# Four gate column units of a streaming encoder step moved from the attention's filling into the paired projection stage

## The chip, the core and the metric

The kernel runs on one core of a Trainium2 chip. The metric is the device time of one launch in microseconds (us). Three runs of the kernel before gave 999.62, 1000.45 and 1001.2 us; the median is 1000.45 us.

## What is computed

One layer of a streaming encoder works on 1024 prompt frames and 64 sample frames (1088 tokens in all) of width 1024. Cut to what matters here:

```python
h = rms_norm(x, norm_w) @ w_in                        # 6144 columns
sq, sk, sv, sz, cq, ck, cv, cz, g_sb, g_cb = split(h)
o_sb = stick_breaking(sq, sk, sv)                     # 8 heads x 64, causal
o_cb = band_attention(norm(cq), norm(ck), cv, bias)   # 8 heads x 64, band of 640 keys
b_sb = (o_sb * silu(sz)) @ w_proj_sb
b_cb = (o_cb * silu(cz)) @ w_proj_cb
y = x + (sigmoid(g_sb) * b_sb + sigmoid(g_cb) * b_cb) @ w_out
```

The two gates g_sb and g_cb have 1024 columns each: columns 4096 to 5119 and 5120 to 6143 of w_in. The weights of the stick-breaking branch (sb) come from a product over the keys that are nearer, those of the band branch (cb) from a softmax over at most 640 keys.

## The kernel before, in words

All tensors are float32. A product of two float32 tensors is done as three matmuls on float32r halves: high by high, high by low and low by high. The helper `Weights` (lines 98 to 130) makes the two halves of a weight block: ScalarE copies the high half (L115), GpSimd subtracts to get the low half (L122).

The order of the work is written out by hand, and every engine takes its instructions in that order. The stages are:

1. **Natural stage** (L464): the columns of cb q, cb k, and both v, with tokens as output rows.
2. **Paired stage** (L593 to L658, matmuls at L634): for each entry of `pairs`, two blocks of 128 columns by all 1088 tokens, in the manner of Strassen and Winograd. The tokens are halved (544 each), the 1024 rows of w_in are halved (512 each), and the two column blocks are the third pair of halves. Seven products of quarters (`right` lists their token operands, some of them sums prepared beforehand in `tms`) stand for the eight of the plain way. `presum` (L389) makes weight sums on VectorE, `prep` (L415) makes the halves (ScalarE L433, GpSimd L434), `emit` (L565) evicts a finished quarter. Each product takes 24 matmuls: 4 blocks of rows, 3 halves, and two pieces of 256 and 288 tokens. So a pair takes 168 matmuls. There are 8 pairs: 4 for sb q and k and 4 of the kind "silu" for z. The kind "sig" is known to `emit`, with a sigmoid by ScalarE and a store by SyncE, and no pair uses it.
3. **Attention**: 144 steps listed in `seq`: branch sb then cb, 4 head pairs p each, tiles t = 8 (the sample), 0 to 7, and two heads hd. The columns of both gates are 16 plain **units** of 128 columns. The generator `run_fill` (L766) issues their matmuls one by one (L773): 3 token chunks of 384, 384 and 320, 8 blocks of rows, 3 halves, 72 matmuls a unit. `fill(n)` takes n matmuls from it. After the units the generator goes on with the sb output projection (`proj_sb`, L873), of which a part is issued within the attention and the rest behind it.
4. **Output**: rest of the sb projection, cb projection (L917), last product (L1409).

One attention step i does, in this order: `qk(i)`, 2 or 4 score matmuls (L1024, L1025) and what reads them; half of the step's fill; `av` (L1115), the product with v, at the steps behind the second head of an odd t or of t = 8; `tr(i - 3)` (LAG is 3), transposes of the weights by TensorE (L1076) into two `pt` buffers, emptied by ScalarE (L1085) or VectorE (L1087) in turn; `mid(i)`; the other half of the fill.

In sb, `qk` lets ScalarE make two sigmoids (L1027, L1028), and `mid` is a scan (L1044) and a product (L1045) on VectorE. In cb, `qk` lets VectorE add the bias to the scores and keep the extreme (L1030, one or two halves), then ScalarE take the exponential with a row sum (L1034); `mid` takes the reciprocal (L1047) and scales (L1048) on VectorE. So in cb VectorE needs ScalarE's exponential of step i before it can finish step i, and in program order it takes up step i + 1 only then.

How many fill matmuls a step gets is planned at L1160 to L1190: six times 24 are issued ahead of the first step; `n_sb` and `n_cb` are then spread over the steps of a branch by weights of n for sb and n + 150 for cb, with n the number of keys of the step. In cb 24 more are given at p = 0, t = 8. For each unit, its weights are split (L115, L122) at the start of the second chunk of the unit before it.

Of the kernel before, what the change touches and what calls it, by code (L numbers as in the profile page):

```python
# [10 lines left out]
AF = mybir.ActivationFunctionType  # L11
# [6 lines left out]
KT = 8  # L18
# [14 lines left out]
def hybrid_step_kernel(ctx: ExitStack, tc: tile.TileContext, x_prompt, x_sample, c_sbk, c_sbv, c_cbk, c_cbv,  # L33
# [47 lines left out]
    d_g = {b: [dram.tile([128, T], F32, name=f"d_g{b}{u}") for u in range(KT)] for b in ("sb", "cb")}  # L81
# [63 lines left out]
    pairs = []  # L145
    for p in (0, 2):
        pairs += [("k", 512 + 128 * p, p), ("q", 128 * p, p)]
    for p in (0, 2):
        pairs += [("silu", 1536 + 128 * p, d_z["sb"][p:p + 2]), ("silu", 3584 + 128 * p, d_z["cb"][p:p + 2])]
    units = [("ev_act", 4096 + 128 * j, (AF.Sigmoid, d_g["sb"][j])) for j in range(KT)]  # L150
    units += [("ev_act", 5120 + 128 * j, (AF.Copy, d_g["cb"][j])) for j in range(KT)]

    def put_t(dst, src):
# [1004 lines left out]
        flush()  # L1158
        f()
    FP = 180  # L1160
    n_sb = 72 * 7
    n_cb = 72 * (len(units) - 9) + FP
    wt = {"sb": lambda n: n, "cb": lambda n: n + 150}
    tot = {b: sum(wt[b](band(b, t)[1]) for bb, p, t, hd in seq if bb == b) for b in ("sb", "cb")}
    amount = {"sb": n_sb, "cb": n_cb}
# [329 lines left out]
```

## Time and profile before

| What | us |
|---|---|
| median of 3 runs | 1000.45 |
| profiled execution, span from first to last instruction | 1000.1 |
| paired stage, 226.65 to 399.06 | 172.4 |
| six fills ahead of the first step, 399.06 to 422.6 | 23.5 |
| attention, sb, 422.6 to 626.2 | 203.6 |
| attention, cb, 626.2 to 846.0 | 219.8 |
| TensorE busy in the whole span | 977.8 |
| VectorE busy | 657.0 |
| ScalarE busy | 472.9 |
| GpSimd busy | 324.9 |

The profile lists no time of the profiled execution besides its span; the span lies 0.35 us under the median of the runs. In the profile PE is TensorE's matmul, PEld its weight load, DVE VectorE, ACT ScalarE, POOL GpSimd and SP SyncE. A matmul's row lists its start and a modelled length that overlaps the next, so the price of a matmul is the distance between starts, or a stretch of the chain divided by its count.

### The profile page before, as it was taken

The numbers are of one execution on the slowest core, as the hardware profiler recorded it, in microseconds if no ns is written. First come the engines' busy times: TensorE is split into PE (matmuls) and PEld (weight loads), VectorE is DVE, ScalarE is ACT, GpSimd is POOL, SyncE is SP. The second block draws the span as 40 slices with busy tenths as digits, with TensorE's granted clock in tenths as the row PEclk, the third lists the DMA queues.
The fourth block names the chain that finished last, engine by engine and source line by source line (L and its number), as shares of the span: only waits on it lengthen the run. The fifth ranks groups of instructions, "written<-read, shape, count | busy, mean of one in ns | idle before, by whom it ended". The sixth has DMA issues, their size and how long they took to land.

```text
span 1000.1 us, 20177 instructions
## 1 busy us (share of the span) xinstructions
PE 977.8 (98%) x7512; PEld 930.8 (93%) x7512; DVE 657.0 (66%) x1233; ACT 472.9 (47%) x1075; POOL 324.9 (32%) x338
## 2 busy tenths in 40 slices
PE   5999999999999999999999999999999899999998
PEld 5999999999999999988898888898989798999998
DVE  5456674895455454099898878565766766499735
ACT  5534443444344433277676656454445434365320
POOL 3276663215445543211111101110202200386552
PEclk9999999999999999999999999999999999999999
DMA  7726577424656332786566544765656854773642
GB/s 237 224 92 221 189 249 256 150 91 150 198 155 192 102 97 85 188 228 187 146 166 159 160 114 117 206 200 152 193 150 186 253 168 147 242 224 101 196 136 89
DMA packets 180865, 169.83 MB, mean 170 GB/s; under 512 B 34912, under 2 KB 167136, under 8 KB 180640
## 3 DMA queue, kind: packets, MB, share of 16 engines
q1 hardware_dynamic: 172048, 160.23, 54.2%
q10 hardware_dynamic: 8720, 8.33, 2.6%
q8 instruction: 59, 0.97, 0.4%
q14 instruction: 38, 0.31, 0.1%
HBM read 109.78 MB, written 58.72 MB: 168 GB/s over the span
## 4 chain that ended last, share of the span: by engine, by line
PE 92%; DMA 2%; DVE 2%; ACT 1%; SPq 1%; issue 1%; POOL 1%; DVEq 0%; ACTq 0%
PE acc L464 19%; PE acc L773 18%; PE b L634 17%; PE b L1409 8%; PE o L1115 7%; PE pt L1076 6%; PE b L917 5%; PE z L1025 3%; PE z L1024 3%; PE acc L873 3%; PE pk L349 1%; DMA wrawx<-in_w_in_dram 1%; DMA gt<-d_gsb 1%; DVE be L1045 1%; PE pt L277 1%
## 5 line engine op out<-in xcount | busy, mean ns | idle before, releaser
L122 POOL TENSOR_TENSOR wlo<-wraw,whi 128x1024 fp32r<-128x1024 f32 x30 | 74.2, 2473 | 243.9 <-ACT whi L115 209.2
L773 PE MATMUL acc<-xm,whi 128*128 128x384 f32 (+1 forms) x384 | 128.5, 335 | 0.0
L1044 DVE TENSOR_TENSOR_SCAN kp<-kp,imp 64x576 f32<-64x576 f32 (+8 forms) x72 | 102.8, 1427 | 21.3 <-ACT kp L1027 21.1
L1034 ACT ACTIVATE be<-be,sm 128x640 f32<-128x640 f32 (+5 forms) x72 | 50.8, 705 | 97.1 <-DVE sm L1030 97.1
L1076 PE MATMUL pt<-ident,be 128*128 128x128 f32 (+2 forms) x608 | 90.1, 272 | 6.4 <-DVE wT L1087 3.4
L1085 ACT ACTIVATE wT<-pt 128x512 f32<-128x512 f32 (+3 forms) x130 | 63.6, 502 | 55.1 <-PE pt L1076 55.1
L1076 PEld LDWEIGHTS pt<-ident,be 128*128 128x128 f32 (+2 forms) x608 | 68.5, 140 | 18.4 <-issue 6.4
L464 PE MATMUL acc<-whi,xa 128*128 128x256 f32 x256 | 74.2, 292 | 0.0
L773 PEld LDWEIGHTS acc<-xm,whi 128*128 128x128 f32 x384 | 72.5, 189 | 1.1
L464 PE MATMUL acc<-wlox,xm 128*128 128x256 f32 x256 | 70.8, 278 | 0.0
L464 PE MATMUL acc<-whi,xm 128*128 128x256 f32 x256 | 70.8, 278 | 0.0
L464 PE MATMUL acc<-wlo,xa 128*128 128x256 f32 x256 | 70.7, 278 | 0.0
L464 PE MATMUL acc<-whix,xb 128*128 128x256 f32 x256 | 70.7, 278 | 0.0
L464 PE MATMUL acc<-whix,xm 128*128 128x256 f32 x256 | 70.6, 278 | 0.0
L1115 PE MATMUL o<-wT,vp 128*64 128x256 f32 (+1 forms) x608 | 66.7, 359 | 0.0
L1045 DVE TENSOR_TENSOR be<-be,kp 64x576 f32<-64x576 f32 (+8 forms) x72 | 60.3, 837 | 9.6
L1027 ACT ACTIVATE kp<-z 128x384 f32<-128x384 f32 (+6 forms) x112 | 54.3, 485 | 24.4 <-PE z L1025 22.9
L773 PE MATMUL acc<-xa,wlo 128*128 128x384 f32 (+1 forms) x192 | 65.4, 341 | 0.0
L773 PE MATMUL acc<-xa,whi 128*128 128x384 f32 (+1 forms) x192 | 65.3, 340 | 0.0
L773 PE MATMUL acc<-xm,wlo 128*128 128x384 f32 (+1 forms) x192 | 65.1, 339 | 0.0
L1115 PEld LDWEIGHTS o<-wT,vp 128*64 128x64 f32 x608 | 42.5, 137 | 23.7 <-issue 7.6
L773 PE MATMUL acc<-xb,whi 128*128 128x384 f32 (+1 forms) x192 | 64.0, 333 | 0.0
(298 smaller groups left out, 3017.2 us busy)
## 6 DMA issues: line engine op xcount, KB each, us to landing
wraw<-in_w_in_dram SPq DMA_DIRECT2D x35, 512.0 KB, 4.7
wrawx<-in_w_in_dram SPq DMA_DIRECT2D x13, 512.0 KB, 4.4
sq<-d_qsbT SPq DMA_DIRECT2D x32, 192.0 KB, 4.7
sq<-d_qcbT SPq DMA_DIRECT2D x32, 192.0 KB, 3.7
gt<-d_gsb SPq DMA_DIRECT2D x30, 192.0 KB, 2.7
xt<-in_x_prompt_dram SPq DMA_DIRECT2D x8, 512.0 KB, 5.1
d_kcbT<-hl SPq DMA_DIRECT2D x8, 512.0 KB, 4.5
d_qcbT<-hl SPq DMA_DIRECT2D x8, 512.0 KB, 5.6
```

Of the source, the lines that this page charges most:

```text
L122: (eng or G).tensor_tensor(out=l, in0=raw, in1=h[:].bitcast(F32), op=OP.subtract)
L464: TE.matmul(ps, x, w, start=m == 0, stop=m == len(steps) - 1)
L634: TE.matmul(ps[:, :m], w[:, hl_, k], right[s](x)[:, k, a:b], start=s < 3 and k == 0 and e == 0, stop=k == 3 and e == 2, skip_group_check=s ...
L773: TE.matmul(ps[:, :b - a], w[:, k], xk(x, k)[:, a:b], start=k == 0 and n == 0, stop=k == KT - 1 and n == 2)
L1027: A.activation(kp[:r, x:y], z[:r, :m], AF.Sigmoid, scale=-0.125)
L1034: A.activation(be[:r, :n], be[:r, :n], AF.Exp, bias=kp[:r, j:j + 1], scale=-1.0, accum_out=kp[:r, 2:3])
L1044: V.tensor_tensor_scan(kp[:r, n - 1::-1], kp[:r, n - 1::-1], im[:, ::-1], 0.0, op0=OP.mult, op1=OP.add)
L1045: V.tensor_tensor(out=be[:r, :n], in0=be[:r, :n], in1=kp[:r, 1:n + 1], op=OP.mult)
L1076: TE.transpose(pt[:kr, x, :r], be[:r, kb * 128:kb * 128 + kr], ident[:r, :r])
L1085: A.activation(w[:, sl:sl + m, q0:q0 + r], pt[:, :m, :r], AF.Copy)
L1115: TE.matmul(o[hd * 64:hd * 64 + 64, c0:c1], vv[:kr, kb, hd * 64:hd * 64 + 64], wT[b, p, j, hd, s // 4][:kr, s % 4, c0:c1], start=si == 0, ...
L1409: TE.matmul(ps[:, t], left[s](xs_, k)[:, ts_], wt_[:, k], start=s < 3 and t == k == e == 0, stop=k == 3 and e == 2, skip_group_check=s > 2 ...
```

## The change

The first four gate units, columns 4096 to 4607 (g_sb, the sigmoid gates j = 0 to 3), become two pairs of the kind "sig" behind the 8 pairs. 12 units are left. The shares of the fill follow: ahead of the first step 144 as before; in sb 36 x 13 = 468 for 504; in cb 72 x 10 - 468 + 180 = 432 for 684. FP stays at 180, so as many matmuls of the sb projection are issued within the attention as before.

```diff
-    units = [("ev_act", 4096 + 128 * j, (AF.Sigmoid, d_g["sb"][j])) for j in range(KT)]
+    NG = 4
+    pairs += [("sig", 4096 + 128 * j, d_g["sb"][j:j + 2]) for j in range(0, NG, 2)]
+    units = [("ev_act", 4096 + 128 * j, (AF.Sigmoid, d_g["sb"][j])) for j in range(NG, KT)]
     units += [("ev_act", 5120 + 128 * j, (AF.Copy, d_g["cb"][j])) for j in range(KT)]
...
     FP = 180
-    n_sb = 72 * 7
-    n_cb = 72 * (len(units) - 9) + FP
+    n_sb = 36 * (len(units) + 1)
+    n_cb = 72 * (len(units) - 2) - n_sb + FP
```

## The prediction

> **What bounds the kernel now.** I read the page first: the span, the busy shares and the chain that ended last.
>
> ```profile
> span 1000.1 us, 20177 instructions
> ...
> PE 977.8 (98%) x7512; PEld 930.8 (93%) x7512; DVE 657.0 (66%) x1233; ACT 472.9 (47%) x1075; POOL 324.9 (32%) x338
> ...
> PE 92%; DMA 2%; DVE 2%; ACT 1%; SPq 1%; issue 1%; POOL 1%; DVEq 0%; ACTq 0%
> ```
>
> TensorE is busy nearly always, and 92% of the chain is its own work. On this reading alone, any saved matmul is saved time. But the change moves work between stages, so I read each stage next (columns: stretch, length, busy time and count of PE, PEld, DVE, ACT and POOL, granted clock, DMA share, GB/s). The first four rows are the stages, the fifth is one pair of heads in cb (its 18 steps), the sixth about one in sb.
>
> ```profile
> 226.65:399.06 172.41, 172.41 (x1385) 171.55 (x1385) 89.14 (x174) 68.41 (x159) 82.67 (x56) 1.00 0.46 140
> 399.06:422.60 23.54, 23.54 (x145) 23.54 (x144) 2.16 (x5) 5.16 (x9) 5.72 (x6) 1.00 0.64 174
> 422.60:626.20 203.60, 200.10 (x1436) 178.27 (x1435) 173.94 (x187) 137.91 (x336) 24.39 (x76) 0.99 0.62 162
> 626.20:846.00 219.80, 216.13 (x1570) 195.21 (x1567) 144.11 (x463) 102.82 (x249) 32.83 (x32) 1.00 0.65 185
> ...
> 681.28:733.99 52.71, 52.71 (x391) 48.01 (x389) 34.29 (x111) 24.46 (x61) 5.60 (x6) 1.00 0.62 170
> ...
> 478.50:529.00 50.50, 50.50 (x365) 44.93 (x365) 43.91 (x49) 34.75 (x86) 6.25 (x20) 1.00 0.62 159
> ```
>
> In the paired stage VectorE, ScalarE and GpSimd each work half the time or less: TensorE alone sets the pace. In sb VectorE is at 85%. In cb it is at 66%, which looks like room. Whether it is room decides this case.
>
> **The paired stage: what is added.** The chain of waits in order of time has two long unbroken stretches of TensorE (start, length, what, count).
>
> ```profile
> 300.67 98.39 PE b L634 x792
> 399.06 23.73 PE acc L773 x144
> ```
>
> A paired matmul costs 98.39 / 792 = 0.1242 us, a plain one 23.73 / 144 = 0.1648 us. Per column of tokens (272 and 362.7 on average) both are 0.456 and 0.454 ns, so seven products for eight is a true saving of TensorE's time. Two pairs are 2 x 168 = 336 matmuls, or **+41.7 us**. Upper bound: an eighth of the stage row, 21.55 a pair, or 43.1; it holds transposes of k that a gate pair has not. Behind the matmuls lie, per pair, 7 splits by ScalarE and GpSimd, 4 sums and some ten evictions by VectorE, two loads of 512 KB and the gate's stores; the eight pairs already did the same at POOL 82.67 of 172.41 and a DMA share of 0.46, so I cost them at nothing. Without that cover the price would be what the busiest of them exceeds TensorE by, and none comes near. The last pairs' stores on SP's queue now stand ahead of the first attention loads; those have 23.5 us of fill as cover as before. Four unit loads, four splits and 12 evictions with their stores leave the attention.
>
> **The attention: what is removed.** Four units are 288 plain matmuls, 288 x 0.1648 = 47.5 us if TensorE paces every step: 36 in sb (5.9 us) and 252 in cb (41.5 us). All in all that would be 47.5 - 41.7 = 5.7 us gained. So what counts is whether TensorE still paces.
>
> *sb, 36 fewer of 504.* Half a matmul a step. In the sb row TensorE waits 203.60 - 200.10 = 3.5 us; VectorE's steps lie close under it (43.91 of 50.50). Its lag is let run over several steps and is caught up at the long av products. Bounds: nothing gained, and 5.9. I take **-3.5**, above the middle, since the row shows TensorE with next to no wait.
>
> *cb, 252 fewer of 684.* A pair of heads now has 684 / 4 = 171 fills; it will have 432 / 4 = 108. TensorE's own work falls from 52.7 to 52.7 - 63 x 0.165 = 42.3 us a pair. Now the other engines. First, TensorE's step at t = 7 today:
>
> ```profile
> 672.45 0.31 PE L1024 MATMUL z<-ks,sq 128*128 128x320 f32 x1
> ...
> 675.67 0.31 PE L1024 MATMUL z<-ks,sq 128*128 128x320 f32 x1
> ...
> 677.39 2.38 PE L1115 MATMUL o<-wT,vp 128*64 128x256 f32 x24
> ```
>
> One step without av is 675.67 - 672.45 = 3.22 us, with 12 fills. It will have 12 x 432 / 684, 7 to 8: about 2.4 us. Second, the step of VectorE and ScalarE, at a place where both were behind, so that nothing in it waits for TensorE:
>
> ```profile
> 721.46 0.48 DVE L1030 CUSTOM_DVE_ANT_0 be<-z,bias 128x320 f32<-128x320 f32 x1
> ...
> 722.75 0.83 ACT L1034 ACTIVATE be<-be,sm 128x640 f32<-128x640 f32 x1 [3.60 <-DVE sm L1030]
> ...
> 723.58 0.58 ACT L1085 ACTIVATE wT<-pt 128x512 f32<-128x512 f32 x1
> 723.70 0.16 DVE L1047 RECIPROCAL sm<-sm 128x1 f32<-128x1 f32 x1 [0.85 <-ACT be L1034]
> 723.90 0.55 DVE L1048 TENSOR_SCALAR be<-be,sm 128x640 f32<-128x640 f32 x1
> 724.37 0.48 DVE L1030 CUSTOM_DVE_ANT_0 be<-z,bias 128x320 f32<-128x320 f32 x1
> ```
>
> This is a **loop between two engines**: VectorE's two reductions, ScalarE's exponential, for which VectorE sits idle 0.85 us, reciprocal, scaling, and only then the next step. It takes 724.37 - 721.46 = 2.91 us however idle the two look in the stage row. Today it hides under 3.22; it doesn't hide under 2.4. The same loop for the other t, by the distance between the first reductions of two steps (t = 8, 8, 0, 0; then t = 1, 2 and 3):
>
> ```profile
> 681.74 0.45 DVE L1030 CUSTOM_DVE_ANT_0 be<-z,bias 64x288 f32<-64x288 f32 x1 [0.21 <-PE z L1025]
> ...
> 684.42 0.44 DVE L1030 CUSTOM_DVE_ANT_0 be<-z,bias 64x288 f32<-64x288 f32 x1
> ...
> 687.09 0.28 DVE L1030 CUSTOM_DVE_ANT_0 be<-z,bias 128x128 f32<-128x128 f32 x1
> ...
> 688.56 0.28 DVE L1030 CUSTOM_DVE_ANT_0 be<-z,bias 128x128 f32<-128x128 f32 x1
> ...
> 639.62 0.42 DVE L1030 CUSTOM_DVE_ANT_0 be<-z,bias 128x256 f32<-128x256 f32 x1 [0.34 <-PE z L1025]
> ...
> 641.37 0.42 DVE L1030 CUSTOM_DVE_ANT_0 be<-z,bias 128x256 f32<-128x256 f32 x1
> ...
> 750.10 0.56 DVE L1030 CUSTOM_DVE_ANT_0 be<-z,bias 128x384 f32<-128x384 f32 x1 [0.43 <-PE z L1025]
> 751.98 0.55 DVE L1030 CUSTOM_DVE_ANT_0 be<-z,bias 128x384 f32<-128x384 f32 x1
> ...
> 702.04 0.68 DVE L1030 CUSTOM_DVE_ANT_0 be<-z,bias 128x512 f32<-128x512 f32 x1
> ...
> 704.21 0.68 DVE L1030 CUSTOM_DVE_ANT_0 be<-z,bias 128x512 f32<-128x512 f32 x1
> ```
>
> 2.68, 1.47, 1.75, 1.88 and 2.17 us. Over a pair of heads: 8 x 2.91 + 2 x (2.68 + 1.47 + 1.75 + 1.88 + 2.17) = **43.2 us**, already more than TensorE's 42.3. The two don't overlap freely: at each av step the loop must wait for TensorE (VectorE's product with z comes behind av), and TensorE may run ahead only until it needs a `pt` buffer, which ScalarE empties behind the exponential. So I add up blocks that end at an av step: lag behind av (0.5), loops of the steps before the last one without av, from that one's reduction to the end of ScalarE's copy (2.7 at 640 keys: 721.46 to 723.58 + 0.58), av (24 in 2.38, 0.1 each), transposes 0.5, half the fill. For t = 6, 7: 0.5 + 2 x 2.91 + 2.7 + 2.4 + 0.5 + 0.6 = 12.5; t = 4, 5 with 16 av: 11.7; t = 8, 0: 0.5 + 2 x 2.68 + 1.4 + 2.4 + 0.5 + 0.2 = 10.4; t = 1 with the 20 short av of the sample, which I put at 1.0: 0.5 + 1.7 + 1.0 + 0.5 = 3.7; t = 2, 3: 0.5 + 2 x 1.88 + 2.1 + 0.8 + 0.9 = 8.1. Together 46.4 us a pair. (For the last step without av at t = 0, 1 and 3 I put its loop, 1.4, 1.7 and 2.1, as an estimate.)
>
> GpSimd's splits come on top, since VectorE now paces:
>
> ```profile
> 675.35 1.11 DVE L1048 TENSOR_SCALAR be<-be,sm 128x640 f32<-128x640 f32 x1
> ...
> 790.56 2.38 POOL L122 TENSOR_TENSOR wlo<-wraw,whi 128x1024 fp32r<-128x1024 f32 x1 [3.81 <-ACT whi L115]
> 790.69 2.60 DVE L1048 TENSOR_SCALAR be<-be,sm 128x640 f32<-128x640 f32 x1
> ```
>
> The scaling of 0.55 us takes 1.11 or 2.60 beside a split: 0.56 to 2.05 us lost each. Of ten splits in cb six are left, 1.5 a pair at 1.3 in the middle: 1.9 us. (The Trainium skill, "SBUF — State Buffer", section "SBUF: two separate sides", has GpSimd and VectorE take one port pair as an exclusive lock for a whole instruction. By it a split could cost 2.4, the pair 3.6 us and the sum 7 us more; the first row speaks for less.) So a pair goes from 52.7 to 48.3, and four give **-17.6**. Bounds: no coupling, 43.2 + 1.5 x 0.56 = 44.0 a pair, -34.8; on the other side 46.4 + 1.5 x 2.05 = 49.5, -12.8; and -41.5 if TensorE paces.
>
> **Sum** against the profiled span: 1000.1 + 41.7 - 3.5 - 17.6 = 1020.7; the median of the runs lies 0.35 higher. Rounded: **1021 us**. Bounds of the terms: 41.7 - 5.9 - 34.8 = +1 and 43.1 - 0 - 12.8 = +30.
>
> **Rivals.** *Loop and TensorE overlap nearly freely*: four `be` buffers and a lag of three steps let TensorE run ahead, 44.0 a pair. That gives +41.7 - 3.5 - 34.8 = +3.4, 1004 us, with a spread of 1002 to 1009. For it: waits of TensorE in cb are few today:
>
> ```profile
> DVE sm L1047 <- ACT be L1034: 16.7, 34, 1.1
> ...
> PE pt L1076 <- ACT wT L1085: 2.0, 2, 1.3
> ...
> PE z L1024 <- DVE sm L1030: 1.4, 2, 1.0
> ```
>
> Against it: those are just the two couplings named, and they show already.
>
> *Faster: TensorE paces cb to the end.* The mechanism is fill as pure surplus: it holds if the loop takes 2.4 us or less a step at 640 keys, in place of 2.91. Then the 5.7 us are gained: 994.4, or 995 by the median. For it speaks the page (98%, 92%); against it the loop's rows.
>
> *The clock falls in the small gaps.* Once before TensorE stood still for 2.40 us, behind a copy that VectorE was late with, and then the clock went down:
>
> ```profile
> 575.38 1.70 PE L1076 MATMUL pt<-ident,be 128*128 128x128 f32 x8 [2.40 <-DVE wT L1087]
> ...
> 574.00:577.50 3.50, 2.12 (x11) 2.12 (x12) 3.37 (x5) 0.98 (x2) 0.29 (x4) 0.74 0.32 95
> ...
> 577.50:580.00 2.50, 2.50 (x17) 1.49 (x18) 0.60 (x2) 0.66 (x3) 0.20 (x2) 0.68 0.00 0
> ```
>
> That cost 0.26 x 3.5 + 0.32 x 2.5 = 1.7 us. Two of the five blocks of each pair with the widest waits and the six splits make 14 such places, 24 us: 1045. Against it: waits of 1.3 and 1.0 left the cb row's clock at 1.00. (The Trainium skill, "TensorE: Matmul & The Clock Gate", section "A second HAM failure mode: psum-queue depth-cycling", says that frequent short idles can make the clock swing; by the section before it only gaps over some 3.4 us do. The 2.40 us here contradict that bound; that short ones swing it no row here shows.)
>
> *The change doesn't do what it says.* Nothing of it depends on data, and the counts follow from the code; what is left is that the seven products are no cheaper, which the price per column excludes. It would leave the time where it is.
>
> **Chances.** My forecast (1010 to 1031) 0.65, free overlap 0.17, TensorE paces 0.08, clock 0.07, nothing 0.03. The range 1003 to 1031 takes in the forecast and nearly all of free overlap and leaves out the rest. A measurement here tells about 0.2% (2 us) from no change. Faster 0.08 (TensorE paces), same 0.05 (nothing, and the low edge of free overlap), slower 0.87.
>
> **What the profile after would show.** Right: the paired stage longer by 41.7 us; sb shorter by up to 5.9; cb some 202 us, not 178; the first reductions at 640 keys 2.9 us apart where no av stands between; TensorE's waits in cb for `pt` (ACT L1085) and for `z` (DVE L1030) grown from 3.7 us to some 25; fewer POOL splits. Wrong: cb at 180 and VectorE still waiting for scores (faster); cb at 185 with its waits at av only (free overlap); a granted clock under 1.00 in many stretches of cb (clock).

## The result, and the profile after

Four runs of the kernel after gave 1015.8 to 1018.47 us, median 1016.93; before, in the same comparison, 1000.83. The ratio is 1.0169 with a 95% interval of 1.0156 to 1.0183: 1.7% slower, where 1021 was forecast. The page of the profile after:

```profile
span 1015.8 us, 20366 instructions
...
PE 983.9 (97%) x7560; PEld 928.0 (91%) x7560; DVE 667.2 (66%) x1261; ACT 479.6 (47%) x1093; POOL 334.3 (33%) x348
...
PE 80%; DVE 8%; DMA 3%; ACT 3%; issue 3%; SPq 2%; POOL 0%; DVEq 0%; ACTq 0%
```

The busy share of TensorE (PE) hardly moved, 98 to 97%, though 15.7 us of span were lost. The third line tells more: TensorE's share of the chain that ended last fell from 92 to 80%, and VectorE (DVE), ScalarE (ACT) and "issue", time in which an engine waited for nothing that the profile shows, took most of its place.

By stages, before and then after. To compare like with like, sb runs from its first score matmul to cb's first, and cb from there to the start of the cb projection; so this cb holds the rest of the sb projection too. Columns as in the prediction.

```profile
226.65:399.06 172.41, 172.41 (x1385) 171.55 (x1385) 89.14 (x174) 68.41 (x159) 82.67 (x56) 1.00 0.46 140
422.63:621.07 198.44, 194.94 (x1403) 173.16 (x1401) 171.83 (x186) 136.19 (x334) 24.39 (x76) 0.99 0.63 164
621.07:865.30 244.23, 239.45 (x1722) 216.84 (x1720) 152.14 (x476) 110.21 (x261) 37.87 (x36) 1.00 0.64 184
...
733.99:789.46 55.47, 54.14 (x391) 48.80 (x389) 36.20 (x114) 28.28 (x71) 11.60 (x12) 1.00 0.65 189
```

```profile
226.07:439.95 213.88, 213.88 (x1722) 213.02 (x1721) 107.87 (x204) 84.17 (x194) 102.25 (x70) 1.00 0.44 134
463.52:658.32 194.80, 190.45 (x1367) 166.94 (x1364) 172.24 (x186) 135.53 (x334) 23.65 (x76) 0.99 0.62 163
658.32:881.00 222.68, 209.60 (x1470) 180.07 (x1469) 144.51 (x476) 101.98 (x246) 28.84 (x32) 0.99 0.65 183
713.77:762.10 48.33, 45.88 (x328) 39.15 (x327) 32.82 (x112) 26.11 (x65) 9.02 (x9) 1.00 0.68 193
762.10:811.79 49.69, 46.23 (x329) 39.11 (x326) 35.78 (x123) 23.55 (x60) 5.91 (x8) 1.00 0.78 216
```

The paired stage took 41.5 us more, sb 3.6 less, cb 21.6 less. The last two rows are the second and the third pair of heads in cb. The second went from 52.71 to 48.33 us, the third from 55.47 to 49.69; with 63 plain matmuls fewer, TensorE's own work fell by 10.4 us in each.

What holds them up is seen in VectorE's rows at 640 keys in cb, the first reduction of four steps in a row; below them TensorE's first score matmul of the same steps.

```profile
736.45 0.48 DVE L1032 CUSTOM_DVE_ANT_0 be<-z,bias 128x320 f32<-128x320 f32 x1
...
739.36 0.48 DVE L1032 CUSTOM_DVE_ANT_0 be<-z,bias 128x320 f32<-128x320 f32 x1
...
742.27 0.48 DVE L1032 CUSTOM_DVE_ANT_0 be<-z,bias 128x320 f32<-128x320 f32 x1
...
745.18 0.48 DVE L1032 CUSTOM_DVE_ANT_0 be<-z,bias 128x320 f32<-128x320 f32 x1
```

```profile
734.81 0.31 PE L1026 MATMUL z<-ks,sq 128*128 128x320 f32 x1
...
737.12 0.31 PE L1026 MATMUL z<-ks,sq 128*128 128x320 f32 x1
...
739.37 0.31 PE L1026 MATMUL z<-ks,sq 128*128 128x320 f32 x1
...
742.14 0.31 PE L1026 MATMUL z<-ks,sq 128*128 128x320 f32 x1
```

VectorE starts a step every 2.91 us to the hundredth. TensorE begins with 2.31 and 2.25 us a step, gets from 1.64 to 2.90 us ahead of the reductions, and then is held: the third step takes 2.77. The waits of cb name the holders (engine and line that waited, for whom, us in all, times, longest):

```profile
DVE sm L1049 <- ACT be L1036: 30.1, 51, 1.1
...
PE z L1026 <- DVE sm L1032: 5.8, 9, 2.0
...
PE pt L1078 <- ACT wT L1087: 5.0, 9, 0.9
```

VectorE's waits for the exponential grew from 16.7 to 30.1 us, and TensorE's two kinds of wait from 1.4 and 2.0 to 5.8 and 5.0. These list only gaps between the modelled ends of matmuls; the whole loss in cb, against a TensorE that gave back every matmul taken away, is 252 x 0.1648 - 21.6 = 20 us.

### The profile page after: what moved, and what is told of

It reads as the page before. It is cut to its first block, busy times and chain, and to the rows that moved or that the text cites. A ratio compares the mean times of both kernels' runs of the same rounds, so it can differ in the third digit from the quotient of the medians.

```text
span 1015.8 us, 20366 instructions
## 1 busy us (share of the span) xinstructions
PE 983.9 (97%) x7560; PEld 928.0 (91%) x7560; DVE 667.2 (66%) x1261; ACT 479.6 (47%) x1093; POOL 334.3 (33%) x348
## 4 chain that ended last, share of the span: by engine, by line
PE 80%; DVE 8%; DMA 3%; ACT 3%; issue 3%; SPq 2%; POOL 0%; DVEq 0%; ACTq 0%
PE b L636 21%; PE acc L466 19%; PE acc L775 10%; PE b L1411 8%; PE o L1117 6%; PE b L919 5%; PE pt L1078 4%; DVE kp L1046 2%; DVE be L1032 2%; PE z L1026 2%; PE z L1027 2%; ACT be L1036 2%; DVE be L1047 1%; DMA gt<-d_gsb 1%; PE acc L875 1%
## 5 line engine op out<-in xcount | busy, mean ns | idle before, releaser
L122 POOL TENSOR_TENSOR wlo<-wraw,whi 128x1024 fp32r<-128x1024 f32 x26 | 63.6, 2446 | 211.1 <-ACT whi L115 162.6
L1078 PE MATMUL pt<-ident,be 128*128 128x128 f32 (+2 forms) x608 | 92.4, 273 | 9.9 <-ACT wT L1087 6.3
L775 PE MATMUL acc<-xm,whi 128*128 128x384 f32 (+1 forms) x288 | 98.1, 341 | 0.0
L1117 PE MATMUL o<-wT,vp 128*64 128x256 f32 (+1 forms) x608 | 75.0, 364 | 1.2 <-ACT wT L1087 0.5
L1117 PEld LDWEIGHTS o<-wT,vp 128*64 128x64 f32 x608 | 46.2, 139 | 28.8 <-issue 7.5
L1047 DVE TENSOR_TENSOR be<-be,kp 64x576 f32<-64x576 f32 (+8 forms) x72 | 62.7, 870 | 9.9 <-ACT sg L750 0.5
L1026 PE MATMUL z<-ks,sq 128*128 128x320 f32 (+4 forms) x192 | 62.7, 329 | 3.9 <-DVE sm L1032 3.8
L1027 PE MATMUL z<-ks,sq 128*128 128x320 f32 (+4 forms) x192 | 62.3, 326 | 0.0
L775 PEld LDWEIGHTS acc<-xm,whi 128*128 128x128 f32 x288 | 54.7, 190 | 1.1
L1030 ACT ACTIVATE be<-z 128x384 f32<-128x384 f32 (+6 forms) x112 | 54.5, 487 | 0.0
L1017 POOL MEMSET kp<- 128x1 f32 (+1 forms) x72 | 6.5, 99 | 130.7 <-DVE be L1047 129.1
```

The costliest lines, as they stand in the source:

```text
L122: (eng or G).tensor_tensor(out=l, in0=raw, in1=h[:].bitcast(F32), op=OP.subtract)
L775: TE.matmul(ps[:, :b - a], w[:, k], xk(x, k)[:, a:b], start=k == 0 and n == 0, stop=k == KT - 1 and n == 2)
L1026: TE.matmul(z[:r, :m], s[:, 2 * hd, q0:q0 + r], ks[:, hd, o + x:o + y], start=True, stop=False)
L1027: TE.matmul(z[:r, :m], s[:, 2 * hd + 1, q0:q0 + r], ks[:, hd, o + x:o + y], start=False, stop=True)
L1047: V.tensor_tensor(out=be[:r, :n], in0=be[:r, :n], in1=kp[:r, 1:n + 1], op=OP.mult)
L1078: TE.transpose(pt[:kr, x, :r], be[:r, kb * 128:kb * 128 + kr], ident[:r, :r])
```

## The experiments

The theory: the loop of VectorE and ScalarE paces cb once the fill is cut. Rivals: GpSimd's splits do it, or a fill matmul has a constant price, or the pairs cost more than their columns. Times are medians; a ratio is to the kernel before in the same comparison.

### The loop cut open: e1 and e2

`mid` of a cb step is issued one step later, behind the next step's reductions, so VectorE has other work while ScalarE makes the exponential. Everything is computed.

```diff
-        if i < len(seq):
+        if i < len(seq) and seq[i][0] == "sb":
             mid(i)
+        if 0 < i <= len(seq) and seq[i - 1][0] == "cb":
+            mid(i - 1)
```

e1, on the kernel after:

> The kernel after, with mid of a cb step (reciprocal and scaling) issued one step later, behind the next step's reductions; sb as it was. Loop theory: VectorE no longer stands idle for the exponential of its own step (30.1 us of such waits in cb), a step at 640 keys takes some 2.1 to 2.4 us of VectorE in place of 2.91 and TensorE's 2.4 paces again. cb falls from 202.9 us towards 183.4 (before's 224.9 less 41.5), with some 4 us of the old waits left: total 997 to 1002. Rival, TensorE waits in cb for pt buffers and GpSimd's splits whatever the order on VectorE: total within 3 us of 1017.

e2, on the kernel before:

> The kernel before with the same delay of mid in cb. Loop theory: TensorE paced cb already, so only its few waits there (3.7 us) can go: 997 to 1000.5. Rival, the order on VectorE costs time at any fill: 15 us or more gained here too.

e1 took 1003.47 us, ratio 1.0021 (1.0009 to 1.0033); e2 999.95, ratio 0.9994 (0.9984 to 1.0003). The same edit gave 13.5 us at the smaller fill and nothing that can be told at the larger one. The profile of e1, the second and third pair of heads:

```profile
710.74:755.52 44.78, 43.69 (x328) 38.24 (x326) 32.97 (x112) 26.19 (x65) 8.69 (x9) 1.00 0.74 205
755.52:800.00 44.48, 43.92 (x329) 38.78 (x327) 36.20 (x123) 23.56 (x60) 5.73 (x8) 1.00 0.85 233
```

and VectorE's rows in it at the same t as above:

```profile
734.39 0.49 DVE L1032 CUSTOM_DVE_ANT_0 be<-z,bias 128x320 f32<-128x320 f32 x1
...
735.50 0.16 DVE L1049 RECIPROCAL sm<-sm 128x1 f32<-128x1 f32 x1
735.70 0.55 DVE L1050 TENSOR_SCALAR be<-be,sm 128x640 f32<-128x640 f32 x1
736.53 0.49 DVE L1032 CUSTOM_DVE_ANT_0 be<-z,bias 128x320 f32<-128x320 f32 x1 [0.28 <-PE z L1027]
```

The reciprocal follows with no wait for ScalarE, and the next step starts after 2.14 us, having waited for TensorE's scores (0.28): here TensorE paces again. (The steps on either side take 2.42 and 2.70 us, all under 2.91.) The loop is shown to be the main cause, 13.5 of the 20 us. e1 ends 1.5 us above its band: some 2 us a pair of heads remain above 42.3.

### The loop made longer: e12 and e13

```diff
             j = len(hs) - 1
+            x = am.tile([128, 256], F32, name="dm", bufs=1)
+            A.activation(x[:r, :min(n, 256)], be[:r, :min(n, 256)], AF.Copy)
             A.activation(be[:r, :n], be[:r, :n], AF.Exp, ...)
```

> The kernel before with one more ScalarE copy (128x256 of be into a scratch tile, not used) between the reductions and the exponential of every cb step: the loop is longer by some 0.35 us at 640 keys, 3.26 in place of 2.91, against TensorE's 3.1 to 3.2. Loop theory: before had that much slack, so little shows: 2 to 8 us slower, 1002 to 1008. Without a loop that waits (ScalarE 47% busy): same as before.

> The kernel after with the same copy. Loop theory: cb runs at the loop's pace but for the av steps, so most of the 72 steps pay: 40 to 60 steps x 0.35 = 14 to 21 us, 1031 to 1038. If cb is paced by something else: 1017 to 1021.

e12, on the kernel before, took 1005.27 us, ratio 1.0037 (1.0024 to 1.0051), as expected; e13, on the kernel after, 1030.51, ratio 1.0276 (1.0251 to 1.0302). So by the medians the same copy cost 4 us before and 13.6 after, just under the band. By the ratios it is 3.7 and 10.7 us, and by the cb rows of the profiles 3.9 (244.23 to 248.12) and 11.7 (222.68 to 234.38). The rows of e13 tell why it is less, VectorE's first reductions at t = 2 to 3 and at t = 4:

```profile
734.37 0.55 DVE L1032 CUSTOM_DVE_ANT_0 be<-z,bias 128x384 f32<-128x384 f32 x1
736.68 0.55 DVE L1032 CUSTOM_DVE_ANT_0 be<-z,bias 128x384 f32<-128x384 f32 x1
...
744.24 0.48 DVE L1032 CUSTOM_DVE_ANT_0 be<-z,bias 128x320 f32<-128x320 f32 x1
747.16 0.48 DVE L1032 CUSTOM_DVE_ANT_0 be<-z,bias 128x320 f32<-128x320 f32 x1
```

At t = 2 the loop grew from 1.88 to 2.31 us. At 640 keys it stayed at 2.92: the copy reads only columns that the first of the two reductions has made, and lies beside the second. My edit did not lengthen the loop where I had counted most of it, so 8 of 18 steps of a pair were longer; the pair from 713.77 on went from 48.33 to 51.06 us, its counterpart before from 52.71 to 52.84. That a longer loop costs little at the large fill and, in the steps where it is longer, most of its length at the small one is what the theory says.

### Half the change: e10

```diff
-    NG = 4
+    NG = 2
...
-    n_sb = 36 * (len(units) + 1)
+    n_sb = 486
```

> Half the change: one gate pair, 14 units, 486 fills in sb and 558 in cb (halfway between before and after). TensorE's step at 640 keys in cb would be 3.22 - 2.2 x 0.17 = 2.8 us, just under the loop's 2.91. Loop theory with a threshold: the first half of the cut in cb is mostly still TensorE's own time: +20.9 - 1.8 - 16 to -18 = +1 to +3, 1001.5 to 1003.5. Rival, a constant price per fill matmul taken away: half of 16.9, 1008.5.

It took 1002.19 us, ratio 1.0006 (0.9996 to 1.0017), as the threshold has it and not the constant price. In its profile the paired stage is 20.6 us longer than before and cb (from the first score matmul, as above) 17.0 shorter, 227.20 for 244.23. The first 126 matmuls taken from cb so gave back 0.135 us each, the next 126 (to 222.68) 0.036 each, where TensorE's own price is 0.165.

### The pairs alone: e3

The two pairs are added and the 16 units kept, so that four units are computed twice.

```diff
+    NG = 4
+    pairs += [("sig", 4096 + 128 * j, d_g["sb"][j:j + 2]) for j in range(0, NG, 2)]
     units = [("ev_act", 4096 + 128 * j, (AF.Sigmoid, d_g["sb"][j])) for j in range(KT)]
...
     n_sb = 72 * 7
     n_cb = 72 * (len(units) - 9) + FP
```

> The kernel before with the two gate pairs added and nothing removed: the four units are computed a second time in the attention, with before's shares of fill. By the price per column 336 x 0.1242 = 41.7 us: 1042.5. If the gate pairs burden the stage or the stores delay the attention, more than 1045.

It took 1043.02 us, ratio 1.0422 (1.0403 to 1.0442): 42.3 us for 41.7. The pairs cost their columns and nothing else that shows beside an interval of 4 us, and taking the four units out of the attention is worth 1043.0 - 1016.9 = 26 us, not 47.5.

### GpSimd's splits: e4, e6, e7

```diff
             wh, wl = W.sp.pop(("u", j))
+            wl = wl or wh
...
-                            W.split(("u", j + 1) if j + 1 < len(units) else ("p", 0))
+                            if j + 1 < len(units):
+                                W.hi(("u", j + 1))
+                            else:
+                                W.split(("p", 0))
```

> The kernel after without GpSimd's subtraction for units 1 to 11 (the high half stands in for the low half, so the gates of these units lose their low-half products' accuracy; the matmul count is the same). As the prediction has it, six splits in cb at 0.56 to 2.05 us each fall due in full, and those in sb partly: 8 us in cb and 2 in sb, total 1005 to 1010. Rival, the splits are hidden beside other waits: above 1014.

e4 took 1009.56 us, ratio 1.0084 (1.0069 to 1.0099): 7.4 us less than the kernel after. That is inside the band, but not where I had put it. sb, and the second and third pair of heads in cb, in e4:

```profile
463.55:652.96 189.41, 186.84 (x1367) 165.71 (x1365) 160.97 (x186) 135.52 (x334) 6.85 (x69) 1.00 0.64 168
...
705.32:753.33 48.01, 45.60 (x327) 39.72 (x326) 32.56 (x112) 26.11 (x65) 6.35 (x8) 1.00 0.70 194
753.33:803.02 49.69, 46.21 (x329) 39.11 (x327) 35.79 (x123) 23.54 (x60) 5.91 (x8) 1.00 0.75 213
```

Between the two profiles, 8.7 us apart, sb gave 5.4 us and cb 3.6 (222.68 to 219.04). In cb the second and third pair stood still: 48.33 to 48.01, and 49.69 both times. 3.1 of the 3.6 us lie in the first pair (55.45 to 52.36), at the passage from sb to cb: there a split had lengthened the last scan of sb from 2.28 to 3.39 us, TensorE stood 2.00 us, and its clock fell behind that; in e4 TensorE's wait there is 0.9 us, and the clock stays at 1.00. So the splits do not pace cb; the rival is out. What they do in sb the profile after shows:

```profile
500.98 2.61 POOL L122 TENSOR_TENSOR wlo<-wraw,whi 128x1024 fp32r<-128x1024 f32 x1 [6.13 <-ACT whi L115]
...
501.26 4.48 DVE L1046 TENSOR_TENSOR_SCAN kp<-kp,imp 128x1024 f32<-128x1024 f32 x1
...
507.82 2.28 DVE L1046 TENSOR_TENSOR_SCAN kp<-kp,imp 128x1024 f32<-128x1024 f32 x1
...
514.26 0.66 PE L1078 MATMUL pt<-ident,be 128*128 128x128 f32 x4 [1.81 <-DVE wT L1089]
...
514.00:516.00 2.00, 1.74 (x13) 1.42 (x15) 1.87 (x3) 0.94 (x3) 0.00 (x0) 0.86 0.76 223
516.00:518.00 2.00, 2.00 (x14) 1.06 (x12) 0.97 (x3) 0.00 (x0) 0.20 (x2) 0.50 0.02 6
518.00:520.00 2.00, 2.00 (x18) 1.26 (x16) 0.00 (x0) 0.00 (x0) 0.00 (x0) 0.78 0.00 0
```

Beside the split a scan over 1024 keys takes 4.48 us, alone 2.28. VectorE is late, TensorE stands 1.81 us for a copy of VectorE's, and then its clock is at 0.50 for some microseconds (the column before the last two). So 2.2 us of VectorE's time become 1.81 us of standing and 0.14 x 2 + 0.50 x 2 + 0.22 x 2 = 1.7 us of slow clock on TensorE.

e6 and e7 have late `mid` and no split, after and before:

> The kernel after with mid of cb one step later and without GpSimd's subtraction for units 1 to 11 (the high half stands in for the low one). Late mid alone gave 1003.5, no split alone 1009.6. If loop and splits are two separate costs: 1003.5 - 7.4 = 996.1. If the splits only cost where the loop leaves no slack in cb: 999 to 1001, from sb alone.

> The kernel before with the same two edits (units 1 to 15 without the subtraction). With both costs of cover taken away, what is left between this and the kernel with both edits and the change is the bare saving of seven products for eight: 47.5 - 41.7 = 5.7 us, less what sb cannot give back (2.3 of its 5.9 us in the kernel after). So this should be 3 to 6 us above the run with the change: 999.5 to 1000 less some us that the splits cost before too, 996 to 1000.

e6 took 997.03 us, ratio 0.9963 (0.9948 to 0.9977), e7 995.92, ratio 0.9953 (0.9938 to 0.9968). The two costs are separate, as expected for e6: 1003.5 - 997.0 = 6.5 us. But e7, just under its band, is on the wrong side of e6: I expected it 3 to 6 us above, and it lies 1.1 below, with intervals that overlap. Even with the loop open and no splits, the change gains nothing that can be told: in the profiles the paired stage and its fill took 42.5 us more than in e7, sb gave 4.8 of its 5.9 us and cb 35.5 of its 41.5.

### The splits in four pieces: e8, e9 and e11

The subtraction of a unit's split goes in four pieces of 128x256, with late `mid`; everything is computed.

```diff
+        for k in range(0, KT, KT // 4):
+            s = slice(k, k + KT // 4)
+            G.tensor_tensor(out=l[:, s], in0=raw[:, s], in1=h[:, s].bitcast(F32), op=OP.subtract)
```

> The kernel after with mid of cb one step later and GpSimd's subtraction for units 1 to 11 in four pieces of 128x256 in place of one of 128x1024; everything is computed. If VectorE is held for the length of a GpSimd instruction, a quarter's length holds it 0.6 us at most at a time: half or more of the 7.4 us of the splits comes back, 997 to 1000, under the kernel before. If the sum of the lengths counts, 1003 as with late mid alone.

> The kernel before with the same two edits. TensorE has most of its cover, but the splits cost a stop of the clock and some waits in sb: 996 to 999.5.

e8, on the kernel after, took 997.55 us, ratio 0.9978 (0.9967 to 0.9989); e9, on the kernel before, 996.13, ratio 0.9955 (0.9940 to 0.9970). Both are a little faster than the kernel before. The pieces gave 5.9 us on top of late `mid` in the kernel after and 3.8 in the kernel before; the scan that took 4.48 us beside a whole split takes 2.83 beside the four pieces. By its median e9 is the best that computes everything, and it does without the change; its interval just touches that of e8. In e8 the whole of cb and its second pair of heads are:

```profile
654.63:860.90 206.27, 199.31 (x1469) 175.71 (x1468) 145.83 (x476) 102.11 (x246) 32.96 (x40) 1.00 0.71 198
705.39:749.90 44.51, 43.43 (x327) 38.29 (x326) 32.74 (x112) 26.21 (x65) 9.63 (x12) 1.00 0.75 209
```

Half the change on top of that:

> Half the change with mid of cb one step later and the splits in four pieces. If the cover is used up gradually, less than a quarter of the whole change's 6 us is lost in cb: 20.9 - 2.4 - 20 = -1.5 beside the kernel before with the same two edits (996.1): 994.5, the fastest. If cb and sb lose in proportion: between 996.1 and 997.6.

e11 took 1000.76 us, ratio 0.9997 (0.9984 to 1.0009): a miss, 6 us above what I expected. Against e9 its paired stage is 20.9 us longer, sb did not get shorter (195.5 for 195.2), and cb got 16.9 shorter. The second pair of heads gave 4.9 us of the 5.2 that TensorE spares, as it should; the third, in which the units end and the projection begins, only 1.3. The chain of waits there is of transfers and their users:

```profile
755.24 3.35 DMA ks<-d_kcbT
...
771.86 3.65 DMA bias<-d_rb
...
778.40 5.46 DMA wraw<-in_w_proj_sb_dram
783.88 2.42 DMA gt<-d_gsb
```

I take from it that a change of the unit count moves this passage to another place of cb, and that this is worth some microseconds either way; e10, with the same 14 units, takes 52.98 us for its third pair, close to e11's 53.19. No run here separates it, so the cause of e11's excess stays open.

## Why the prediction was right, point by point

**The paired stage.** Forecast +41.7, measured +41.5 in the stage rows and 42.3 by e3. The price per column held (0.457 ns by its own division, not 0.456; nothing hangs on it), and the work behind the matmuls hid, as costed at nothing.

**sb.** Forecast -3.5, measured -3.6, but the agreement is partly luck. e4 changes sb by 5.4 us with not one fill matmul fewer; e10 takes only 18 away and gains the same 3.6 (198.44 to 194.83), with the fall of the clock gone; e11 takes 18 away and gains nothing. The size depends on where a split meets a scan and whether the clock falls for it, once in sb both before and after.

**cb, the loop.** Right in its mechanism: 2.91 us a step, VectorE's waits for the exponential at 30 us, the cure by e1, the threshold by e10. The size was wrong twice, in opposite directions. The step "GpSimd's splits come on top, 1.9 us a pair" was mis-sized: e4 has 0.3 and 0.0. The step "together 46.4 us a pair" was too low: without splits the pairs take 48.0 and 49.7. Together they gave 48.3 a pair, and 48.33 was measured for the second: that the two errors cancel is luck. One sign named ahead did not come as said: TensorE's two waits in cb were to grow from 3.7 us to some 25, and they came to 10.8.

**cb, the total.** Forecast -17.6, measured -21.6. I had worked with the quietest pair of before (52.7) and a gain of 4.4 us for all four. The first three gave 4.8, 4.4 and 5.8 us, and the fourth with the rest of the sb projection 6.6. The third and fourth hold the passage to the projection; that this passage is why they gave more is not shown by a run.

**The rivals.** TensorE pacing to the end is out. *The loop and TensorE overlap nearly freely* is out, by TensorE's third step above and by the pairs, which take 48.33 and 49.69 us where it had 44.0. *The clock falls in the small gaps*: cb's many waits of up to 0.9 us left the clock at 1.00; it fell once at the passage from sb to cb behind a wait of 2.00 us that goes back to the bias loads, and once in sb, where the rival had put 14 such places. The profile of e13 has both falls as well; the profiles of the runs with no split or with pieces have none, and neither has e10, with its splits whole.

**What stays open.** Of the 5.7 us that seven products for eight should bring, nothing that can be told came even in e6 and e8, against e7 and e9. In e8 cb gave 35.7 of 41.5 us against e9; TensorE still waits there for `pt` buffers that ScalarE empties, 4.2 us against 2.1. That accounts for part of the 6 us that cb kept; the rest wasn't settled.

## What to carry to other kernels

Work that fills gaps is worth only the time by which the host stage then still follows the same engine: before taking filler away, find the longest chain that one step must run through on the other engines (here 2.91 us against TensorE's 3.22), since idle time inside such a loop looks like room in a busy share of 66% and isn't. If the loop can be opened by issuing a step's tail behind the next step's head, do that first. And look for the gain of half a change: here the first half of the cut in cb gave nearly four times what the second did.

## What the runs showed of the hardware that I had not expected

The clock can fall after short stops: in the kernel after it went to 0.50 behind waits of TensorE of 1.81 and 2.00 us, before behind one of 2.40. The length of the wait alone does not decide it. In e1 the clock fell 0.7 us after the end of a wait of 0.91 us (first two rows) and stayed at 1.00 through one of 1.84 us (last two rows); in e6 it stayed at 1.00 through one of 1.74 us.

```profile
467.30:470.70 3.40, 2.49 (x21) 2.01 (x20) 3.13 (x6) 1.99 (x9) 0.20 (x2) 1.00 0.87 238
470.70:474.10 3.40, 3.40 (x28) 2.84 (x28) 2.17 (x6) 1.11 (x5) 0.20 (x2) 0.50 1.02 248
514.00:516.00 2.00, 0.16 (x3) 0.01 (x1) 1.87 (x4) 0.76 (x2) 0.10 (x1) 1.00 0.62 158
516.00:518.00 2.00, 2.00 (x17) 1.59 (x19) 1.87 (x2) 0.94 (x3) 0.00 (x0) 1.00 0.58 170
```

(The Trainium skill, "TensorE: Matmul & The Clock Gate", section "HAM oscillation — how this bites in real kernels", sets idle gaps over some 3.4 us as the limit; the clock fell here behind waits of 0.91 to 2.40 us.)

One split of 2.61 us cost a scan beside it 2.2 us. (The Trainium skill, "SBUF — State Buffer", section "SBUF: two separate sides", has GpSimd and a VectorE instruction with two inputs in SBUF exclude one another for a whole instruction; the 4.48 us agree with it.) Cutting the splits into four pieces took 5.9 us from the kernel after with late `mid`, and the profile with pieces has no fall of the clock between 420 and 880 us.
